# Loads of x traced inside another block, and one down group of layer 0 with two instead of three pairs in seven products

## The chip, the core and the metric

One core of a Trainium2 chip runs the whole program in one launch. The metric is the device time of one execution in microseconds (us). Most executions of a kernel lie close together; the three runs of the kernel before lie between 2137.33 and 2138.62 us, with a median of 2138.08 us.

The core has five engines with a queue of instructions each: TensorE (PE, matrix products), VectorE (DVE), ScalarE (ACT), GpSimd (POOL) and SyncE (SP, which here issues the loads of the weights). Each queue is worked off in its order, and an instruction at the head that waits holds everything behind it.

## The reference, cut to what matters

Two layers on 256 tokens of width 2048, in float32. Each layer is RMSNorm, a mixer and a residual add, then RMSNorm, a SwiGLU feed-forward and a residual add. Layer 0 mixes by sliding-window attention and an mLSTM, layer 1 by forgetting attention.

```python
for layer in range(DEPTH):
    xn = rms_norm(h, norm_mix[layer])
    mix = swa_mlstm_mixer(xn, ...) if layer % 2 == 0 else forgetting_attention_mixer(xn, ...)
    h = h + mix
    h = h + swiglu(rms_norm(h, norm_ffn[layer]), w_gate[layer], w_up[layer], w_down[layer])
return rms_norm(h, norm_final)

def swiglu(xn, w_gate, w_up, w_down):
    return (jax.nn.silu(xn @ w_gate) * (xn @ w_up)) @ w_down
```

The hidden width of the feed-forward is 5632. All weights are read from memory once, mostly 512 KB at a time.

## The kernel before, in words

**Three matmuls per product.** A float32 operand is split into a rounded part `hi` and a rest `lo`, and each product becomes three matmuls (L356 to L358, or L177 to L179 in the plain loop `gemm`): hi by xh, lo by xh, hi by xl. A weight chunk of 256 rows by 512 columns (two blocks of 128 rows, here two k's) is loaded by SP into a tile `raw` (L104), cast on ACT to `hi` (L149), and DVE forms `lo = raw - hi` (L150). `raw` tiles come from two pools of four buffers: `wr` for chunks that are only cast, and the pool `fp` of the layer for chunks of the pairs described next. `hi` and `lo` have six buffers each.

**Seven products for eight.** In the feed-forward, `pair_group` (from L373) works on two column blocks of weights at once, over a list of pairs of k's. The list (`ORDER` or `DOWN`) says for every pair whether it is plain (kind 0) or not (kind 1). A plain pair has two k's, two column blocks and two halves of 128 tokens: eight products, 24 matmuls. A pair of kind 1 forms seven products from sums of the operands: 21 matmuls, but DVE also makes `t4` (L394, L395), two blocks of `raw` (L399, L400) and splits of these (`ht`, `lt`, L251 and L252) with ACT. Four of the seven products collect in four accumulators of their own, `prods`. Behind the last pair of kind 1 these are folded once for the group: ACT copies one (L420), DVE makes `u2` and three rows of `c` (L421 to L424). What is plain collects in four other accumulators, `plain`.

**The down projection** of a part is two calls of `pair_group`, n0 = 0 and n0 = 2, for output columns 0 to 1023 and 1024 to 2047. The last part of a layer has sixteen k's, so `DOWN[8]`: eight pairs, those with numbers 2, 4 and 6 of kind 1. After each call DVE adds `c` to the residual `h` (L538, four adds of 128x512), and `close` adds the `plain` accumulators (`add_out`, L257, four adds), TensorE transposes the new `h` (`split_scaled`, L229, eight per column block of 512), ACT and DVE scale and split the transposes into `xh` and `xl` (L234, L235), and ACT forms the sums of squares (`square_sum`, L200). The next layer's first projection reads these `xh` and `xl`: its k's 0 to 7 come from the call n0 = 0, its k's 8 to 15 from the call n0 = 2. This first projection has 272 columns, the ones behind it 512.

**Order.** Python only traces the instructions. A list scheduler then orders every engine's queue by its own estimate of when operands are ready, so matmuls of the next layer's first projection stand among and behind the last of a down group. `tc.issue_after(ins)` puts each instruction of its block that runs on the same engine as `ins` behind it in that engine's queue. It sets an order and no wait. `latest[0]` is the last cast of a weight chunk, on ACT (L149).

**The start.** SP loads the transposed input in four pieces (L114) with the first four weight chunks between them, then the input itself into `h` in four pieces (L564), then weights. The squares of `h` (L200) follow on ACT. The projections `acc0` (k and v) and `acc1` (the first of q, L563 to L566) run on PE.

Of the kernel before, what the change touches and what calls it, by code (L numbers as in the profile page):

```python
# [23 lines left out]
NB = 512  # L24
# [13 lines left out]
    6: ((0, 0), (0, 1), (1, 2), (0, 3), (1, 4), (0, 5)),  # L38
    8: ((0, 0), (0, 1), (1, 2), (0, 3), (1, 4), (0, 5), (1, 6), (0, 7)),
}  # L40
MID = 6
MID_DOWN = 5
RAWS = 4
# [10 lines left out]
def trunk(  # L54
# [20 lines left out]
    nc = tc.nc  # L75
# [34 lines left out]
    h = cp.tile([P, NT, D], F32, name="h")  # L110
    xv = x[0].rearrange("(t p) d -> p t d", p=P)
# [28 lines left out]
    latest = [None]  # L140

    def load_chunk(w, k0, c0, n):
        raw = ahead.pop(0) if ahead else load_raw(w, k0, c0, n)
        return split_chunk(raw, n)
# [10 lines left out]
    def new_acc():  # L155
        return [pa.tile([P, NB], F32, tag="acc", name="acc") for _ in range(NT)]
# [6 lines left out]
    def gemm(acc, lhs, w, c0, n, k_from, k_to, k_all, skew=1):  # L163
        k0 = k_from
        while k0 < k_to:
            last = k_to == k_all and k0 + skew * CK >= k_all
            chunks = [load_chunk(w, kc, c0, n) for kc in range(k0, k_all if last else k0 + CK, CK)]
            order = [(i, t) for i in range(len(chunks) * CK) for t in range(NT)]
            if last:
                order.sort(key=lambda it: it[1])  # L170
            for i, t in order:
                k = k0 + i
                hi, lo = (c[:, i % CK, 0:n] for c in chunks[i // CK])
                ah, al = lhs(k)
                ts = slice(t * P, (t + 1) * P)
                o = acc[t][:, 0:n]
                nc.tensor.matmul(o, ah[:, ts], hi, start=(k == 0), stop=False)  # L177
                nc.tensor.matmul(o, ah[:, ts], lo, start=False, stop=False)  # L178
                nc.tensor.matmul(o, al[:, ts], hi, start=False, stop=(k == k_all - 1))  # L179
            k0 += len(chunks) * CK  # L180
# [14 lines left out]
    def square_sum(key, n):  # L195
        if n == 0:
            sums[key] = sm.tile([P, NT, 4], F32, tag="ss", name="ss")
        for t in range(NT):
            junk = sm.tile([P, NB], BF16, tag="junk", name="junk", bufs=1)
            nc.scalar.activation(  # L200
                junk, h[:, t, n * NB : (n + 1) * NB], AF.Square, accum_out=sums[key][:, t, n : n + 1]
            )

    def rstd(key):
        tot = sm.tile([P, NT], F32, tag="tot", name="tot")
        nc.vector.reduce_sum(tot, sums[key], axis=AX)
        nc.vector.tensor_scalar(tot, tot, 1.0 / D, EPS, op0=ALU.mult, op1=ALU.add)
        r = sm.tile([P, NT], F32, tag="r", name="r")
        nc.gpsimd.tensor_tensor(out=r, in0=tot, in1=mhalf[:, 0:NT], op=ALU.pow)
        return r  # L210
# [216 lines left out]
    def ffn(layer, fp, sx, sd, key, idx_next=None, key_next=None, finish=None):  # L427
# [6 lines left out]
        for g0, g1 in zip(PARTS, PARTS[1:]):  # L434
            end = g1 == PARTS[-1]
            nk = 4 * (g1 - g0)
            order = DOWN[nk // 2]
            todo = []
            for g in range(g0, g1):
# [4 lines left out]
                todo = []  # L444
# [53 lines left out]

                todo = [(MID if g < g1 - 1 else MID_DOWN, join)]

# [4 lines left out]
            def close(acc, n):  # L505
                if not end:
                    add_out(acc, n)
                elif idx_next is None:
                    finish(acc, n, gf)
                else:  # L510
                    add_out(acc, n)
                    split_scaled(idx_next, n)
                    square_sum(key_next, n)

            gf = None
            wd = w_down[layer][4 * g0 * P : 4 * g1 * P, :]
            for n0 in (0, 2):
                if end and idx_next is None and n0 == 2:
                    for n in (2, 3):
                        acc = new_acc()  # L520
                        gemm(acc, m_of, wd, n * NB, NB, 0, nk, nk, skew=3 if n == 3 else 1)
                        close(acc, n)
                    continue
                plain, c = pair_group(
                    fp, 1 - n0 // 2, m_of, sums_d, [(wd, n0 * NB), (wd, (n0 + 1) * NB)], order, todo
                )
                todo = []
                if end and idx_next is None:
                    gf = [fp.tile([P, CK, NB], F32, tag="raw", name="gf", bufs=RAWS) for _ in range(2)]
                    for i in range(2):  # L530
                        nc.gpsimd.dma_start(
                            gf[i].rearrange("p a n -> p (a n)"),
                            norm_final[i * CK * NB : (i + 1) * CK * NB].partition_broadcast(P),
                        )
                for m in range(2):
                    for t in range(NT):
                        o = h[:, t, (n0 + m) * NB : (n0 + m + 1) * NB]
                        nc.vector.tensor_tensor(out=o, in0=c[:, 2 * m + t, :], in1=o, op=ALU.add)  # L538
                for m in range(2):
                    close(plain[m], n0 + m)  # L540

    def close_layer(layer, w_out, idx, key, **rest):
        with tc.tile_pool(name=f"fp{layer}", bufs=2) as fp:
            nx = len(mixed_of(ORDER))
            nd = max(len(mixed_of(o)) for o in DOWN.values())
            sx = [fp.tile([P, nx, 4, P], F32R, name=f"sx{i}", bufs=1) for i in range(2)]
            sd = [fp.tile([P, nd, 4, P], F32R, name=f"sd{i}", bufs=1) for i in range(2)]
            out_proj(w_out, idx, key, (*sx, fp))
            ffn(layer, fp, sx, sd, key, **rest)
# [11 lines left out]
    early.close()  # L561
    acc1 = new_acc()
    for n in range(4):  # L563
        nc.sync.dma_start(h[:, :, n * NB : (n + 1) * NB], xv[:, :, n * NB : (n + 1) * NB])  # L564
        gemm(acc1, x_of, wi, OFF_QS, NB, 4 * n, 4 * n + 4, KT)
        square_sum("m0", n)  # L566
    r = rstd("m0")
    with tc.tile_pool(name="ev", bufs=1) as ev:
# [413 lines left out]
```

## Time and profile before

| | us |
|---|---|
| median of three runs | 2138.08 |
| lowest and highest | 2137.33, 2138.62 |
| the profiled execution, its own time | 2137.85 |
| its span, first to last instruction | 2136.1 |
| ACT busy in it | 1253.7 |
| DVE busy in it | 1713.8 |

The profile is of one execution. "Busy" for PE counts a matmul until its modelled end, and matmuls overlap, so what matters is the distance between their starts. In a row of a timeline the columns are start, duration, engine, line, operation, out<-in with shapes, a count, and in brackets the idle time before it and what ended that. A row with a count above one stands for several instructions in a row. In the view of waits the columns are who waited, for whom, total us, times and the longest. The granted clock is the share of its full clock that TensorE was given.

### The profile page before, as it was taken

To read this page: it belongs to the slowest core of one execution; us is meant where nothing else is said; L and a number is where in the kernel's file an instruction comes from. 1 tells how busy PE (TensorE), PEld (TensorE's weight loads), DVE (VectorE), ACT (ScalarE), POOL (GpSimd) and SP (SyncE) were. 2 spreads that over 40 slices of the span, in tenths; PEclk is the share of its full clock that TensorE was granted. 3 is DMA by queue.
4 is the path that set the end of the run, shared out by engine and by line. 5 is a ranking of instruction groups with operands and counts; after the bars stand their busy time and mean duration, and the time that the engine had idled before them with its cause. 6 is when DMAs were issued, how large, how long until landed. Compare 5 with 4: busy or idle time off the path is not lost.

```text
span 2136.1 us, 26792 instructions
## 1 busy us (share of the span) xinstructions
PE 2109.5 (99%) x9705; PEld 1752.1 (82%) x9705; DVE 1713.8 (80%) x2210; ACT 1253.7 (59%) x1594; POOL 36.7 (2%) x61
## 2 busy tenths in 40 slices
PE   7999999999999999999999999999999999999998
PEld 6888888888888888888888888888888888888886
DVE  5666567899999999999755555768899998999995
ACT  6475455665477646766545444556655667556763
POOL 2010000000000000000010000000000000000000
PEclk9999999999999999999999999999999999999999
DMA  8455556665677666766475664756766767666764
GB/s 288 137 161 163 170 188 202 203 216 181 213 211 218 211 201 212 221 214 197 139 232 165 177 177 132 235 175 187 225 198 202 233 189 208 229 201 205 223 205 135
DMA packets 257846, 420.95 MB, mean 197 GB/s; under 512 B 56449, under 2 KB 64689, under 8 KB 257585
## 3 DMA queue, kind: packets, MB, share of 16 engines
q1 hardware_dynamic: 256832, 415.49, 62.9%
q0 software_dynamic: 736, 3.71, 0.6%
q8 instruction: 76, 1.25, 0.2%
q14 instruction: 58, 0.47, 0.1%
q10 hardware_dynamic: 144, 0.03, 0.0%
HBM read 406.57 MB, written 2.11 MB: 191 GB/s over the span
## 4 chain that ended last, share of the span: by engine, by line
PE 97%; DMA 1%; DVE 1%; ACT 1%; issue 0%; SPq 0%; POOLq 0%; POOL 0%; DVEq 0%; ACTq 0%
PE acc L356 16%; PE acc L357 16%; PE acc L358 16%; PE acc L179 11%; PE acc L178 10%; PE acc L177 10%; PE prod L358 4%; PE prod L356 4%; PE prod L357 4%; PE p L280 1%; PE ptm L263 1%; PE po L331 1%; DMA xc<-in_xt_dram 1%; PE pt L229 1%; DMA raw<-in_w_up_dram 0%
## 5 line engine op out<-in xcount | busy, mean ns | idle before, releaser
L149 ACT CAST hi<-raw 128x1024 fp32r<-128x1024 f32 (+2 forms) x681 | 694.7, 1032 | 583.2 <-PE acc L179 257.7
L150 DVE TENSOR_TENSOR lo<-raw,hi 128x1024 fp32r<-128x1024 f32 (+2 forms) x681 | 809.8, 1201 | 249.3 <-ACT hi L149 247.7
L357 PE MATMUL acc<-lo,xh 128*128 128x512 f32 x946 | 368.4, 389 | 0.0
L356 PE MATMUL acc<-hi,xh 128*128 128x512 f32 x946 | 365.3, 390 | 0.3 <-DVE u L421 0.2
L358 PE MATMUL acc<-hi,xl 128*128 128x512 f32 x946 | 363.5, 389 | 0.0
L177 PE MATMUL acc<-hi,xh 128*128 128x512 f32 (+3 forms) x736 | 277.7, 380 | 12.1 <-ACT hi L149 12.1
L178 PE MATMUL acc<-lo,xh 128*128 128x512 f32 (+3 forms) x736 | 277.8, 378 | 0.6 <-DVE lo L150 0.5
L179 PE MATMUL acc<-hi,xl 128*128 128x512 f32 (+3 forms) x736 | 278.3, 379 | 0.0
L356 PEld LDWEIGHTS acc<-hi,xh 128*128 128x128 f32 x946 | 177.6, 188 | 37.9 <-DVE u L421 1.1
L358 PEld LDWEIGHTS acc<-hi,xl 128*128 128x128 f32 x946 | 177.6, 188 | 36.9
L357 PEld LDWEIGHTS acc<-lo,xh 128*128 128x128 f32 x946 | 177.6, 188 | 36.6
L357 PE MATMUL acc<-lo,mh 128*128 128x512 f32 x437 | 170.5, 390 | 0.0
L177 PEld LDWEIGHTS acc<-hi,xh 128*128 128x128 f32 x736 | 140.5, 191 | 36.2 <-ACT hi L149 12.8
L358 PE MATMUL acc<-hi,ml 128*128 128x512 f32 x437 | 168.6, 390 | 0.0
L356 PE MATMUL acc<-hi,mh 128*128 128x512 f32 x437 | 167.4, 390 | 0.0
L178 PEld LDWEIGHTS acc<-lo,xh 128*128 128x128 f32 x736 | 140.7, 191 | 25.6 <-DVE lo L150 1.7
L179 PEld LDWEIGHTS acc<-hi,xl 128*128 128x128 f32 x736 | 140.6, 191 | 25.7 <-issue 1.7
L251 ACT CAST ht<-raw 128x1024 fp32r<-128x1024 f32 x95 | 99.8, 1051 | 52.1 <-issue 20.8
L252 DVE TENSOR_TENSOR lt<-raw,ht 128x1024 fp32r<-128x1024 f32 x95 | 115.9, 1220 | 16.2 <-ACT ht L251 15.9
L177 PE MATMUL acc<-hi,mh 128*128 128x512 f32 x320 | 125.8, 393 | 1.2 <-ACT mh L251 1.2
L178 PE MATMUL acc<-lo,mh 128*128 128x512 f32 x320 | 125.8, 394 | 0.0
L179 PE MATMUL acc<-hi,ml 128*128 128x512 f32 x320 | 124.1, 390 | 0.0
(307 smaller groups left out, 3089.6 us busy)
## 6 DMA issues: line engine op xcount, KB each, us to landing
raw<-in_w_gate_dram SPq DMA_DIRECT2D x176, 512.0 KB, 4.5
raw<-in_w_up_dram SPq DMA_DIRECT2D x176, 512.0 KB, 4.7
raw<-in_w_down_dram SPq DMA_DIRECT2D x176, 512.0 KB, 4.8
raw<-in_w_in_odd_dram SPq DMA_DIRECT2D x88, 512.0 KB, 3.8
raw<-in_w_in_even_dram SPq DMA_DIRECT2D x64, 512.0 KB, 4.4
raw<-in_w_out_even_dram SPq DMA_DIRECT2D x32, 512.0 KB, 3.8
raw<-in_w_out_odd_dram SPq DMA_DIRECT2D x32, 512.0 KB, 4.0
raw<-in_w_in_odd_dram SPq DMA_DIRECT2D x8, 272.0 KB, 3.0
```

Of the source, the lines that this page charges most:

```text
L149: latest[0] = nc.scalar.copy(hi[:, :, 0:n], raw[:, :, 0:n])
L150: nc.vector.tensor_tensor(out=lo[:, :, 0:n], in0=raw[:, :, 0:n], in1=hi[:, :, 0:n].bitcast(F32), op=ALU.subtract)
L177: nc.tensor.matmul(o, ah[:, ts], hi, start=(k == 0), stop=False)
L178: nc.tensor.matmul(o, ah[:, ts], lo, start=False, stop=False)
L179: nc.tensor.matmul(o, al[:, ts], hi, start=False, stop=(k == k_all - 1))
L229: nc.tensor.transpose(pt[:, i, t, :], h[:, t, k * P : (k + 1) * P], ident)
L251: nc.scalar.copy(dst_h, src)
L252: nc.vector.tensor_tensor(out=dst_l, in0=src, in1=dst_h.bitcast(F32), op=ALU.subtract)
L263: nc.tensor.transpose(pt[:, i, :], s_, ident)
L356: nc.tensor.matmul(o, ah, hi, start=start, stop=False)
L357: nc.tensor.matmul(o, ah, lo, start=False, stop=False)
L358: nc.tensor.matmul(o, al, hi, start=False, stop=stop)
```

## The change

Two edits. In the projection `acc1` the load of a quarter of x into `h` is traced behind the matmuls of that quarter, in a block `tc.issue_after(latest[0].ins)`, where before it was traced ahead of them. And the call n0 = 2 of the last down group of layer 0 gets a list of its own, `DOWN_END`, in which pair 6 is plain: pairs 2 and 4 stay in seven products. (Layer 1's last group does not take this path for n0 = 2.)

```diff
+DOWN_END = ((0, 0), (0, 1), (1, 2), (0, 3), (1, 4), (0, 5), (0, 6), (0, 7))
...
                 plain, c = pair_group(
-                    fp, 1 - n0 // 2, m_of, sums_d, [(wd, n0 * NB), (wd, (n0 + 1) * NB)], order, todo
+                    fp,
+                    1 - n0 // 2,
+                    m_of,
+                    sums_d,
+                    [(wd, n0 * NB), (wd, (n0 + 1) * NB)],
+                    DOWN_END if end and n0 == 2 else order,
+                    todo,
                 )
...
     for n in range(4):
-        nc.sync.dma_start(h[:, :, n * NB : (n + 1) * NB], xv[:, :, n * NB : (n + 1) * NB])
         gemm(acc1, x_of, wi, OFF_QS, NB, 4 * n, 4 * n + 4, KT)
+        with tc.issue_after(latest[0].ins):
+            nc.sync.dma_start(h[:, :, n * NB : (n + 1) * NB], xv[:, :, n * NB : (n + 1) * NB])
         square_sum("m0", n)
```

The activation sums of pair 6 are still made, since the call n0 = 0 uses them.

## The prediction

> **What bounds the kernel now.** I read the page first, then the view of PE's waits, then the timelines of PE and DVE where that view points.
>
> ```profile
> PE 2109.5 (99%) x9705; PEld 1752.1 (82%) x9705; DVE 1713.8 (80%) x2210; ACT 1253.7 (59%) x1594; POOL 36.7 (2%) x61
> PE 97%; DMA 1%; DVE 1%; ACT 1%; issue 0%; SPq 0%; POOLq 0%; POOL 0%; DVEq 0%; ACTq 0%
> ```
>
> PE is busy 99% of the span, and the chain that ended last runs 97% over PE. So time changes only where PE gets more or fewer matmuls, or where one of its few waits goes. All waits of PE:
>
> ```profile
> PE acc L177 <- ACT hi L149: 12.1, 2, 7.6
> PE pt L229 <- DVE h L257: 3.8, 1, 3.8
> PE acc L177 <- ACT mh L251: 1.2, 1, 1.2
> PE acc L178 <- DVE lo L150: 0.5, 1, 0.5
> PE acc L356 <- DVE u L421: 0.2, 1, 0.2
> ```
>
> The first row is the start. The second is one wait of 3.8 us: transposes of the new residual wait for DVE's add. It lies at the end of layer 0's last down group, where the second edit is. PE there:
>
> ```profile
> 1035.63 0.39 PE L356 MATMUL acc<-hi,mh 128*128 128x512 f32 x1
> ...
> 1036.76 0.39 PE L358 MATMUL acc<-hi,ml 128*128 128x512 f32 x1
> ...
> 1037.86 0.28 PE L177 MATMUL acc<-hi,xh 128*128 128x272 f32 x1
> ...
> 1038.48 0.29 PE L179 MATMUL acc<-hi,xl 128*128 128x272 f32 x1
> ...
> 1042.23 0.39 PE L358 MATMUL prod<-ht,sd 128*128 128x512 f32 x1
> ...
> 1044.27 0.27 PE L229 MATMUL pt<-ident,h 128*128 128x128 f32 x1
> 1048.36 1.54 PE L229 MATMUL pt<-ident,h 128*128 128x128 f32 x6 [3.82 <-DVE h L257]
> 1049.56 0.57 PE L177 MATMUL acc<-hi,xh 128*128 128x272 f32 x1
> ...
> 1053.55 0.43 PE L179 MATMUL acc<-hi,xl 128*128 128x272 f32 x1
> 1053.78 0.53 PE L229 MATMUL pt<-ident,h 128*128 128x128 f32 x2
> 1054.06 0.38 PE L177 MATMUL acc<-hi,xh 128*128 128x272 f32 x1
> ```
>
> Starts give the pitch. From 1035.63 to 1036.76 lie five steps: 0.226 us for a matmul of 512 columns. From 1037.86 to 1038.48 lie five steps: 0.124 us for 272 columns. Behind the wait the same 272-column matmuls, eighteen from 1049.56 to 1053.55, stand 0.235 us apart. TensorE runs there at about half pace, as the granted clock says:
>
> ```profile
> 1040.00:1050.00 10.00, 6.18 (x31) 5.19 (x31) 7.00 (x12) 2.07 (x5) 0.00 (x0) 0.86 0.35 98
> 1050.00:1060.00 10.00, 10.00 (x65) 9.88 (x65) 8.27 (x15) 8.96 (x17) 0.69 (x1) 0.80 0.58 168
> ```
>
> The clock is the third number from the right: 0.86, then 0.80. So the wait costs twice. From 1044.27 to 1054.06 PE does 9 transposes and 18 matmuls in 9.79 us. At full pace the transposes take 0.11 us each (row below, six in 0.66) and the matmuls 0.124 us, together 9 x 0.11 + 18 x 0.124 = 3.22 us. The loss is **6.57 us**: some 3.9 of standing still and 2.7 of half pace.
>
> ```profile
> 1054.69 0.66 PE pt L229 x6
> ```
>
> Why DVE is late:
>
> ```profile
> 1042.66 0.69 DVE L421 TENSOR_TENSOR u<-prod,c 128x512 f32<-128x512 f32 x1 [3.57 <-PE prod L358]
> ...
> 1045.19 1.28 DVE L538 TENSOR_TENSOR h<-c,h 128x512 f32<-128x512 f32 x2
> 1046.39 0.72 DVE L150 TENSOR_TENSOR lo<-raw,hi 128x544 fp32r<-128x544 f32 x1
> 1047.02 0.68 DVE L538 TENSOR_TENSOR h<-c,h 128x512 f32<-128x512 f32 x1
> 1047.62 1.88 DVE L257 TENSOR_TENSOR h<-acc,h 128x512 f32<-128x512 f32 x3
> ```
>
> DVE had idled 3.57 us for the last product of pair 6 (PE's row at 1042.23, ended 1042.62). Only then can it fold the products and add, one 0.6 us step behind the other. PE has 1.7 us of matmuls left at that point.
>
> **The second edit, part by part.** With pair 6 plain, the issue lists of the two built programs are the same on PE up to the matmul at
>
> ```profile
> 1024.98 0.39 PE L356 MATMUL prod<-hi,mh 128*128 128x512 f32 x1
> ```
>
> and part there. From there to the group's last matmul before has 71 matmuls of the group, with 24 of the next projection strewn in; after has 74 in one piece. *Added:* 3 matmuls, 3 x 0.226 = **0.68 us**. Bounds: 0.68 if PE never waits, 0 if they fill a wait; I take 0.68.
>
> *Moved:* the last matmul that goes into the four products is now the 50th of those 74, for pair 4 ends it. It starts at 1024.98 + 49 x 0.226 = 1036.05 and ends at about 1036.45, where before it was 1042.62. DVE can fold at 1036.5. In its new list, from `u` (L421) to the last add stand 13 steps: ten folds and adds and three 272-column splits among them. By the rows above the first add came 2.53 us behind `u`, and that add with the eight steps behind it, at 0.6 to 0.64 us each, ends 8.1 us behind `u`, at 1044.6. PE finishes the group at 1024.98 + 74 x 0.226 = 1041.7. Then its list has 2 transposes (their adds and product buffers are through by 1039.1), 24 matmuls of 272 columns (to 1044.9), 2 transposes, 8 matmuls (to 1046.1), then the transposes that need the add of the third step from the end (1043.4), and near 1047.4 those that need the last add (1044.6). Every wait is over some 2.7 us ahead. **What is late next:** the splits `xl` of the new k's, for the matmuls near 1049.9, which by the same walk are ready about 2 us ahead, and the later ones 1.1 us ahead. If the cast buffers come free in the least lucky order (all held to 1041.9), DVE's chain shifts by 2.3 us and PE loses about 0.5 us there.
>
> *Removed from DVE and ACT:* the weight sums of pair 6, four DVE steps of 0.6 and two splits, two ACT casts; a 512-column split and cast grow to 1024. Neither engine is on the path but for the chain above, so this is worth nothing by itself.
>
> *Loads:* pair 6's second chunk and pair 7's two move to other buffers of the pool `wr`, in the same queue order.
>
> ```profile
> 1006.83 3.31 SPq L104 DMA_DIRECT2D raw<-in_w_down_dram  x3
> ...
> 1015.58 0.37 SPq L104 DMA_DIRECT2D raw<-in_w_in_odd_dram  x1
> ...
> 1018.10 0.37 SPq L104 DMA_DIRECT2D raw<-in_w_in_odd_dram  x1
> DMA to landing us min/median/max: 2.8/3.5/5.3
> L149 ACT CAST hi<-raw 128x1024 fp32r<-128x1024 f32 x2 | 2.0, 1050 | 2.9 <-issue 2.9
> L150 DVE TENSOR_TENSOR lo<-raw,hi 128x1024 fp32r<-128x1024 f32 x6 | 7.2, 1218 | 2.6 <-ACT hi L149 2.6
> ```
>
> Before, the three issues from 1006.83 held both chunks of pair 7. After, these take the buffers that are now freed for the issues at 1015.58 and 1018.10. With the longest landing of 5.3 us they are there by 1020.9 and 1023.4, cast (1.05) and split (1.22) by 1026 at the latest. PE needs the first at 1024.98 + 26 x 0.226 = 1030.9. About 5 us are to spare, so I cost this at nothing.
>
> **The first edit.** `issue_after` sets an order on the engine of the instruction it names, which is ACT. The loads of x are issued by SP. The list of the built program shows them at rows 9 to 12 of SP's queue with the same waits, ahead of all weights of this projection, before and after. A wait on the casts could not stand there, as the casts' own weights queue behind. ACT's list is the same too: the eight squares still precede the casts.
>
> ```profile
> 5.16 7.08 SPq L564 DMA_DIRECT2D h<-in_x_dram  x4
> 19.07 0.62 ACT L200 ACTIVATE junk<-h 128x512 bf16<-128x512 f32 x1
> 24.97 1.98 ACT L149 CAST hi<-raw 128x1024 fp32r<-128x1024 f32 x2
> ```
>
> Were the squares (19.07 to 24.97) to leave the casts' way, up to 5.9 us would go; were each of four loads to stop the queue for one landing, up to 4 x 5.3 = 21 us would come. I take 0, since the order is unchanged.
>
> **Sum.** Against the profiled execution (span 2136.1, its time 2137.85): -6.57 + 0.68 = -5.9 us, a span near 2130.2. The median 2138.08 is 0.2 above the profiled one; from it I predict **2132.2 us**.
>
> **A rule weighed.** The half pace lasted from 1048.36 to 1054.06, 5.7 us, after a gap of 3.8 us. The Trainium skill, "TensorE: Matmul & The Clock Gate", section "What's actually happening", says that about 3.4 us without work halve the clock, about 3.4 us of sustained work restore it, and that the windows run freely. By its figure the half pace would cost an estimated 1.7 us, not 2.7, and the sum would be 2133.2; the trace's rows decide, and I keep 2.7.
>
> **The rivals.**
> - *Another wait takes the place.* DVE's chain holds three splits, each behind an ACT cast that waits for a buffer PE frees. If these or `xl` come later than walked, PE waits again at the transposes or at the first new k's: against it stand margins of 1.1 to 2.7 us, for it that I infer the buffers. A new wait of 1 to 4 us gives 2133.2 to 2136.2, say 2134.5.
> - *The clock was lost in the profiled run only.* If the halving depends on where a 3.8 us gap falls, the runs behind the median may not have paid the 2.7 us, and only 3.9 - 0.7 = 3.2 us go: 2134.9. By the rule of free windows of some 3.4 us (the Trainium skill, same page and section) it would be so, since a gap of 3.8 us seldom holds a whole window. Against it: the profiled run at 2137.85 lies within three runs that spread by 1.3 us, less than 2.7.
> - *Slower: pair 7's weights arrive late.* They are issued up to 8.8 us later than before (1006.83 to 1015.58). Cast and split (2.3 us) must end by 1032.3 for the second, issued at 1018.1, so from a landing time of about 12 us PE stops and each further us costs one; past 18 us the 5.9 us gained are eaten. At 20 us, with the half pace of 2.7 us behind it, 2143. Landings in this window are at most 5.3 us.
> - *The first edit acts after all*, in a way that the lists don't show: -5.9 to +21 us by the bounds above, say 2128.
>
> **Chances.** Forecast 0.73; another wait 0.12; clock 0.06; late weights 0.05; first edit 0.04. A measurement here can tell about 0.2%, 4.3 us, from no change. Faster: nearly all of the forecast (0.71), a third of another wait (0.04) and half of the first edit (0.02), 0.77. Same: 0.02 + 0.08 + 0.06 = 0.16. Slower: late weights and the other half, 0.07. The forecast's own range is 2130.9 (the three matmuls cost nothing, or a run at the low end of the scatter of 0.7) to 2133.4 (0.5 lost at `xl`, scatter). To hold 8 in 10 it reaches into the first rival: 2130.9 to 2134.6.
>
> **What would show it.** In the profile after: PE's wait of 3.8 us is gone from the view of waits; the clock is 1.00 in the stretch from 1030 to 1060; PE has three matmuls more; DVE's `u` of this group starts near 1036.5; the start to 35 us is as before. A PE wait of over 1 us near 1042 to 1052, or a clock below 1, makes the first rival; a median near 2135 with no wait left makes the second.

## The result, and the profile after

| | before | after |
|---|---|---|
| median of nine runs each, one chip, us | 2137.33 | 2132.1 |
| lowest and highest, us | 2136.32, 2138.62 | 2131.22, 2132.69 |
| span of the profiled execution, us | 2136.1 | 2130.8 |

The ratio of after to before is 0.9975, with an interval of 0.9965 to 0.9985: about 0.25% faster, 5.2 us by the medians and 5.3 us by the spans. The forecast was 2132.2 us, by a gain of 5.9.

The page's row of engines and its chain that ended last, for the kernel after:

```profile
PE 2108.0 (99%) x9708; PEld 1749.6 (82%) x9708; DVE 1709.9 (80%) x2204; ACT 1252.5 (59%) x1592; POOL 35.7 (2%) x61
PE 98%; DMA 1%; ACT 1%; DVE 0%; issue 0%; SPq 0%; DVEq 0%; POOLq 0%; POOL 0%; ACTq 0%
```

PE has 9708 matmuls where it had 9705: the three that a plain pair 6 adds. DVE has six instructions fewer (four weight sums, two splits), ACT two casts fewer. PE's busy time is nonetheless 1.5 us lower with three matmuls more, because a matmul at half pace counts as longer. The waits of PE, all of them (line numbers are one higher than before up to L525, seven or eight higher behind that):

```profile
PE acc L178 <- ACT hi L150: 12.4, 2, 7.5
PE acc L178 <- ACT mh L252: 1.2, 1, 1.2
PE acc L357 <- DVE u L422: 0.3, 1, 0.3
PE acc L179 <- DVE lo L151: 0.2, 1, 0.2
```

The row of 3.8 us (`pt` behind DVE's `h`) is gone and no row has come in its place. The stretches of the kernel after around that place; the clock is the third number from the right:

```profile
1030.00:1040.00 10.00, 10.00 (x46) 8.29 (x45) 6.04 (x9) 2.94 (x5) 0.00 (x0) 1.00 0.22 63
1040.00:1050.00 10.00, 10.00 (x75) 9.52 (x74) 8.77 (x18) 7.37 (x17) 0.69 (x1) 1.00 0.63 166
1050.00:1060.00 10.00, 10.00 (x68) 9.31 (x67) 7.86 (x10) 6.74 (x9) 0.00 (x0) 1.00 0.90 261
```

Before, PE was busy 6.18 of the ten us behind 1040 and the clock read 0.86 and then 0.80. Now PE is busy throughout and the clock is 1.00. Timelines of the kernel after, DVE first, then PE:

```profile
1037.12 0.69 DVE L422 TENSOR_TENSOR u<-prod,c 128x512 f32<-128x512 f32 x1 [3.39 <-PE prod L359]
...
1042.72 1.28 DVE L258 TENSOR_TENSOR h<-acc,h 128x512 f32<-128x512 f32 x2
...
1044.55 0.69 DVE L258 TENSOR_TENSOR h<-acc,h 128x512 f32<-128x512 f32 x1
```

```profile
1025.58 0.39 PE L357 MATMUL prod<-ht,sd 128*128 128x512 f32 x1
...
1036.69 0.39 PE L359 MATMUL prod<-ht,sd 128*128 128x512 f32 x1
...
1042.13 0.39 PE L359 MATMUL acc<-hi,ml 128*128 128x512 f32 x1
1042.36 0.38 PE L230 MATMUL pt<-ident,h 128*128 128x128 f32 x2
...
1046.81 0.82 PE L230 MATMUL pt<-ident,h 128*128 128x128 f32 x6
...
1048.10 0.82 PE L230 MATMUL pt<-ident,h 128*128 128x128 f32 x6
```

DVE still idles 3.39 us for the last of the four products, but that product now ends at 1037.08 and not at 1042.62, with 24 matmuls of 512 columns still to run. The add that the transposes at 1046.81 need ends at 1044.00, the last add at 1045.24 against transposes at 1048.10: some 2.8 us of margin at both.

To separate this place from the rest of the run I take two marks on PE that every kernel here has: the first transpose of the group before (near 1000) and the first transpose `pp` of layer 1 (near 1214). Before, then after:

```profile
999.75 0.27 PE L229 MATMUL pt<-ident,h 128*128 128x128 f32 x1
...
1219.61 0.27 PE L323 MATMUL pp<-ident,s 128*128 128x128 f32 x1
```

```profile
1000.36 0.27 PE L230 MATMUL pt<-ident,h 128*128 128x128 f32 x1
...
1214.19 0.27 PE L324 MATMUL pp<-ident,s 128*128 128x128 f32 x1
```

From mark to mark before takes 219.86 us and after 213.83: 6.03 us are gained between these marks. The spans differ by 5.3 only, since after is 0.61 us late already at the first mark. The edits did not do this: the second acts behind that mark, and the kernel with the first edit alone (e1 below, whose queues are those of before) reaches it at 1000.34. What made after late shows in stretches of one us near 195 us, first of before, then of after:

```profile
195.00:196.00 1.00, 1.00 (x8) 0.70 (x7) 1.00 (x6) 0.77 (x3) 0.00 (x0) 1.00 0.53 203
```

```profile
195.00:196.00 1.00, 1.00 (x5) 0.82 (x5) 1.00 (x3) 0.90 (x4) 0.00 (x0) 0.77 0.08 16
...
198.00:199.00 1.00, 1.00 (x6) 1.00 (x5) 0.95 (x1) 0.01 (x1) 0.00 (x0) 0.53 0.00 0
```

In after the clock is at half from 195.54 to 198.94, and by the profile PE is busy in the whole stretch and in the 3.4 us ahead of it; in before the clock stays at 1.00 there. The same matmuls start 0.81 us earlier in after than in before ahead of this stretch (191.24 against 192.05) and 0.78 us later behind it (199.50 against 198.72). So a half-clock stretch can come without a gap, and not in every execution: e1 has this one too, with the queues of before.

### The profile page after: what moved, and what is told of

Its sections match the earlier page's. It is cut to its first block, busy times and chain, and to the rows that moved or that the text cites. A ratio compares the mean times of both kernels' runs of the same rounds, so it can differ in the third digit from the quotient of the medians.

```text
span 2130.8 us, 26787 instructions
## 1 busy us (share of the span) xinstructions
PE 2108.0 (99%) x9708; PEld 1749.6 (82%) x9708; DVE 1709.9 (80%) x2204; ACT 1252.5 (59%) x1592; POOL 35.7 (2%) x61
## 4 chain that ended last, share of the span: by engine, by line
PE 98%; DMA 1%; ACT 1%; DVE 0%; issue 0%; SPq 0%; DVEq 0%; POOLq 0%; POOL 0%; ACTq 0%
PE acc L357 17%; PE acc L358 17%; PE acc L359 17%; PE acc L180 11%; PE acc L178 11%; PE acc L179 10%; PE prod L357 4%; PE prod L358 4%; PE prod L359 4%; PE ptm L264 1%; PE p L281 1%; PE po L332 1%; DMA xc<-in_xt_dram 1%; PE pt L230 0%; PE pp L324 0%; PE p L274 0%
```

## The experiments

The theory under test: the second edit gives the whole gain, because the last product of the last pair of kind 1 comes early enough for DVE's chain to end before PE needs it, and the first edit does nothing. Rivals: the first edit has a part in it; the gain is less work on DVE or other loads, not the place of the last product; the half pace is a fixed price of the wait, or it is a matter of chance.

### Each edit alone

**e1**, the first edit only:

```diff
-                    DOWN_END if end and n0 == 2 else order,
+                    order,
```

> The first edit alone, the down group as before. Theory (the order block binds only instructions of ACT, and the loads of x are SP's): every queue stands as before, so the time is that of before, near 2137.3 us, with the start to 35 us unchanged. Rival (the loads of x move after all): a time at least 1 us away from before, with another start.

Measured: 2137.36 us, ratio to before 1.0001 [0.9992, 1.001]. The order of every engine's queue is that of the kernel before. The first edit is inert.

**e2**, the second edit only (the loads of x traced ahead of the matmuls as before):

> The second edit alone, the loads of x traced where they were. Theory (all of the gain comes from the end of layer 0): the time of the changed kernel, 2132.1 us, 5.2 below before. Rival (the two edits share it): a time between 2133 and 2137.

Measured: 2132.25 us, ratio 0.9978 [0.9969, 0.9987]; after was 2132.1. The second edit is the whole change. From mark to mark e2 takes 213.84 us:

```profile
1000.13 0.27 PE L230 MATMUL pt<-ident,h 128*128 128x128 f32 x1
...
1213.97 0.27 PE L324 MATMUL pp<-ident,s 128*128 128x128 f32 x1
```

The profile of e1 shows one thing more. It does the same work as the kernel before and waits as long at the same place, yet it lost less there:

```profile
PE pt L230 <- DVE h L258: 3.8, 1, 3.8
```

```profile
1000.34 0.27 PE L230 MATMUL pt<-ident,h 128*128 128x128 f32 x1
...
1044.87 0.27 PE L230 MATMUL pt<-ident,h 128*128 128x128 f32 x1
1048.96 1.54 PE L230 MATMUL pt<-ident,h 128*128 128x128 f32 x6 [3.82 <-DVE h L258]
...
1053.23 0.38 PE L230 MATMUL pt<-ident,h 128*128 128x128 f32 x2
1053.37 0.37 PE L178 MATMUL acc<-hi,xh 128*128 128x272 f32 x1
...
1218.92 0.27 PE L324 MATMUL pp<-ident,s 128*128 128x128 f32 x1
```

From 1044.87 to 1053.37 are 8.50 us for the same nine transposes and 18 matmuls that took 9.79 us in the profile before, and mark to mark are 218.58 us, not 219.86. The wait is 3.82 us in both; what differs is how long the clock stayed at half. One-us stretches show its edges, first of before, then of e1:

```profile
1047.00:1048.00 1.00, 0.00 (x0) 0.00 (x0) 1.00 (x3) 0.00 (x0) 0.00 (x0) 0.63 0.00 0
...
1054.00:1055.00 1.00, 1.00 (x10) 1.00 (x10) 0.06 (x1) 0.98 (x1) 0.00 (x0) 0.96 0.79 117
```

```profile
1048.00:1049.00 1.00, 0.04 (x1) 0.05 (x1) 1.00 (x3) 0.01 (x1) 0.00 (x0) 0.69 0.30 23
...
1051.00:1052.00 1.00, 1.00 (x7) 1.00 (x7) 0.50 (x2) 1.00 (x4) 0.00 (x0) 0.61 0.01 4
```

All stretches between read 0.50. A mean of 0.63 over one us is 0.26 us at full clock and 0.74 at half, so before was halved from 1047.26 to 1054.08 (0.96 leaves 0.08 at half), 6.82 us; e1, in the same way, from 1048.38 to 1051.78, 3.40 us. One is twice the other.

### How early the last product has to be

**e3**, pair 2 alone of kind 1 (three more matmuls than after, and the last product earlier still):

```diff
-DOWN_END = ((0, 0), (0, 1), (1, 2), (0, 3), (1, 4), (0, 5), (0, 6), (0, 7))
+DOWN_END = ((0, 0), (0, 1), (1, 2), (0, 3), (0, 4), (0, 5), (0, 6), (0, 7))
```

> The list of the last down group of layer 0 with pair 2 alone in seven products, pairs 4 and 6 plain. Theory (the gain is the wait, which is gone already; each plain pair costs three matmuls of 0.226 us): 0.7 us above the changed kernel, about 2132.8. Rival (the gain comes from less work on DVE, of which more now goes): below the changed kernel, about 2130.

Measured: 2132.56 us, ratio 0.9979 [0.997, 0.9988], 0.3 us above e2 and 0.5 above after. From mark to mark (999.75 to 1214.37) it takes 214.62 us, 0.79 above after: the three matmuls cost what 3 x 0.226 = 0.68 says, near enough, and nothing is gained by being earlier than after already is. Nor does still less work on DVE gain anything, as the rival had it.

**e4**, three pairs of kind 1, placed earlier in the list:

```diff
+DOWN_END = ((0, 0), (1, 2), (0, 1), (1, 4), (0, 3), (1, 6), (0, 5), (0, 7))
```

> All three pairs in seven products, but at places 1, 3 and 5 of eight, with two plain pairs behind the last. Theory (what matters is how many matmuls stand behind the last product that goes into the sums, not how many pairs are in seven): no PE wait at the transposes, three matmuls less than the changed kernel, 0.7 us below it, about 2131.4. Rival (three pairs of kind 1 make DVE late wherever they stand): a wait of 2 to 4 us is back and the time is 2134 to 2138.

Measured: 2133.26 us, ratio 0.9981 [0.9972, 0.999], where 2131.4 was expected. The scheduler still puts the products of pair 6 late, with 14 matmuls of 512 columns of the group behind the last of them (8 before, 24 after), and PE waits. The waits of e4, and its clock in the ten us in which it does:

```profile
PE pt L230 <- DVE h L258: 1.1, 1, 1.1
```

```profile
1040.00:1050.00 10.00, 8.95 (x59) 8.02 (x57) 9.03 (x16) 4.73 (x12) 0.00 (x0) 1.00 0.45 123
```

No half clock came with a wait of 1.1 us: the clock stays 1.00.

**e5**, pair 6 of kind 1 at the place of pair 5:

```diff
+DOWN_END = ((0, 0), (0, 1), (1, 2), (0, 3), (1, 4), (1, 6), (0, 5), (0, 7))
```

> Three pairs in seven products at places 2, 4 and 5, two plain pairs behind them. Theory (matmuls behind the last product decide): between before and the changed kernel; pair 4 and pair 6 follow each other, so DVE makes the sums of pair 6 under pressure; if the last product ends 2 us earlier than in before, the wait shrinks from 3.8 to about 1.8 us and the half pace goes, about 2133.5 us. Rival (the scheduler puts the same matmuls last whatever the list says): 2137, as before.

Measured: 2136.1 us, ratio 0.9993 [0.9984, 1.0002], where about 2133.5 was expected. About three quarters of the gain is gone. PE waits 2.5 us, in its timeline here, and the clock is halved from 1049.24 to 1052.64, 3.40 us, by the one-us stretches behind it:

```profile
1047.82 0.87 PE L230 MATMUL pt<-ident,h 128*128 128x128 f32 x6 [2.46 <-DVE h L258]
```

```profile
1049.00:1050.00 1.00, 1.00 (x8) 1.00 (x7) 1.00 (x4) 1.00 (x4) 0.00 (x0) 0.62 0.88 270
...
1052.00:1053.00 1.00, 1.00 (x8) 1.00 (x7) 0.99 (x2) 1.00 (x2) 0.26 (x1) 0.68 0.81 98
```

The transposes at 1047.82 still ran at full pace (0.87 us for six, in e1 1.54), so here the halving came while PE was working again.

The number of matmuls alone does not decide, as the theory had it: e4 and e5 both have 14 of 512 columns behind the last product, and wait 1.05 and 2.46 us. What differs is the time that PE can fill. From the start of the last product to the first transpose it is 2.04 us in before, 3.40 in e5 and 4.58 in e4, where nine matmuls of the next projection stand there as well. With the waits (3.82, 2.46 and 1.05) the sums are 5.86, 5.86 and 5.63 us. In after PE has 5.67 us there and does not wait.

### A later DVE with the new list

If the margin at the adds is what matters, the new list with more work on DVE must wait again. **e6** and **e7** add 8 and 12 steps ahead of the adds; each takes the maximum of a row of `c` with itself, which leaves it as it is:

```diff
+                if end and n0 == 2:
+                    for _ in range(8):
+                        nc.vector.tensor_tensor(out=c[:, 1, :], in0=c[:, 1, :], in1=c[:, 1, :], op=ALU.max)
                 for m in range(2):
```

> The changed kernel with eight steps of 0.6 us (a maximum of one row of c with itself) put on DVE ahead of the residual adds of the last down group of layer 0. DVE's adds come 4.8 us later, against some 2.7 us of cover: a PE wait of about 2 us at the transposes. Theory (half pace comes only behind a wait of over some 3 us): the wait alone is lost, about 2134.1 us, granted clock 1.00 behind it. Rival (every wait is followed by half pace in proportion, 0.7 us for each us): about 2135.5, clock below 1.

> The same with twelve such steps: adds 7.2 us later, a PE wait of about 4.4 us. Theory: the wait and a half pace of about 2.7 us behind it, about 2139.2 us, clock near 0.8 in the 10 us behind the wait. Rival (no half pace, the 2.7 us of before had another cause): about 2136.5, clock 1.00.

Measured: e6 2138.64 us, ratio 1.0007 [0.9997, 1.0016], where 2134.1 was expected; e7 2142.51 us, ratio 1.0023 [1.0014, 1.0033], where 2139.2 was expected. The scheduler spread the steps among DVE's other work, so the wait came later than meant and others of 0.8 to 1.0 us came with it. What gates PE is the same pair of lines. PE's transposes at the wait in e6, then in e7:

```profile
1056.82 1.50 PE L230 MATMUL pt<-ident,h 128*128 128x128 f32 x6 [2.02 <-DVE h L258]
```

```profile
1059.27 1.54 PE L230 MATMUL pt<-ident,h 128*128 128x128 f32 x6 [4.92 <-DVE h L258]
```

The edges of the half clock in e6:

```profile
1056.00:1057.00 1.00, 0.18 (x1) 0.18 (x2) 0.73 (x2) 0.20 (x1) 0.00 (x0) 0.95 0.50 188
...
1060.00:1061.00 1.00, 1.00 (x6) 0.77 (x5) 1.00 (x3) 0.78 (x3) 0.69 (x1) 0.84 0.00 0
```

It lasts from 1056.90 to 1060.32, 3.42 us, behind a wait of only 2.0 us. My expectation that half pace follows only waits of more than about 3 us is refuted. In e7 the same reading gives 1056.60 to 1063.44, 6.84 us. So the new list is fast because DVE's chain is through in time; late DVE steps alone bring the wait and the half clock back, and take the whole gain (e6, whose interval holds 1) or more (e7).

### The loads of x where they do act

The first edit names a cast on ACT, so it cannot move a load on SP. **e8** names the last weight load instead:

```diff
+    loaded = [None]
...
-        nc.sync.dma_start(
+        loaded[0] = nc.sync.dma_start(
...
-        with tc.issue_after(latest[0].ins):
+        with tc.issue_after(loaded[0].ins):
```

> The changed kernel with the four loads of x really moved: each is put behind the last weight load of its quarter in SP's queue (the block names the load, not the cast). The squares on ACT then follow the casts. Theory (the PE wait of 4.9 us near 21 us is there because the casts stand behind the eight squares and their weights behind the loads of x): that wait and the half pace behind it shrink, 3 to 8 us below the changed kernel, 2124 to 2129. Rival (the start is bound by what must be loaded, whatever its order, or the later scale factors make the heads wait): within 1 us of the changed kernel, or above it.

Measured: **2125.2 us**, ratio to before 0.994 [0.9928, 0.9953], 6.9 us below after. This is the fastest version by its median; its five executions lie between 2122.92 and 2126.21 us. SP's queue in the kernel after, then in e8:

```profile
5.12 7.13 SPq L573 DMA_DIRECT2D h<-in_x_dram  x4
13.30 0.61 SPq L105 DMA_DIRECT2D raw<-in_w_in_even_dram  x1
```

```profile
8.91 14.34 SPq L107 DMA_DIRECT2D raw<-in_w_in_even_dram  x6
23.30 0.46 SPq L575 DMA_DIRECT2D h<-in_x_dram  x1
```

In after, four loads of x stand ahead of the weights that `acc1` needs; in e8, six weight loads go first. The first 35 us of after and of e8:

```profile
0.00:35.00 35.00, 22.27 (x75) 16.47 (x76) 18.83 (x30) 23.93 (x44) 12.38 (x31) 0.90 0.92 307
```

```profile
0.00:35.00 35.00, 27.28 (x109) 21.86 (x110) 20.46 (x28) 21.72 (x34) 14.53 (x30) 1.00 0.91 311
```

PE runs 109 matmuls there, not 75. After waits 4.93 us for a cast up to 26.07, and its mean clock of 0.90 stands for 7 of the 35 us at half; e8 has neither. The DMA engines are as busy in both (0.92 and 0.91): the same bytes, in an order that PE can use.

**e9** moves the squares of `h` on ACT behind the casts instead, and leaves the loads in front:

```diff
+        nc.sync.dma_start(h[:, :, n * NB : (n + 1) * NB], xv[:, :, n * NB : (n + 1) * NB])
         gemm(acc1, x_of, wi, OFF_QS, NB, 4 * n, 4 * n + 4, KT)
         with tc.issue_after(latest[0].ins):
-            nc.sync.dma_start(h[:, :, n * NB : (n + 1) * NB], xv[:, :, n * NB : (n + 1) * NB])
-        square_sum("m0", n)
+            square_sum("m0", n)
```

> The changed kernel with the loads of x back ahead, and the squares on ACT, instead of the loads, traced in the block that names the cast (the same engine, so the order holds). ACT then casts the weights of the first projection of q before it squares x. Theory (both orders matter at the start: 5.9 us of squares, and weights that land late behind four loads of x): part of the gain of the kernel with the loads moved, about 2128 to 2131 us. Rival (the loads' order alone makes the start): within 0.5 us of 2132.1.

Measured: 2131.0 us, ratio 0.9972 [0.9961, 0.9984], 1.1 us below after. The executions of the two overlap (2130.03 to 2132.06 here, 2131.22 to 2132.69 for after), so this is a small gain at most. The cast no longer stands behind squares, but then it waits for its weights; ACT in e9:

```profile
23.75 1.04 ACT L150 CAST hi<-raw 128x1024 fp32r<-128x1024 f32 x1 [4.75 <-DMA raw<-in_w_in_even_dram]
```

It starts at 23.75, where before it started at 24.97, and PE waits 3.45 us for it and 0.53 for a split, where after waited 4.93. So the loads of x hold the weights, and that is most of what e8 removes.

**e10** is e8 with the old list, and **e11** is e8 with three pairs of kind 1 placed earlier still:

```diff
-DOWN_END = ((0, 0), (0, 1), (1, 2), (0, 3), (1, 4), (0, 5), (0, 6), (0, 7))
+DOWN_END = ((0, 0), (1, 2), (1, 4), (0, 1), (1, 6), (0, 3), (0, 5), (0, 7))
```

> The loads of x really moved, with the old list (three pairs, at places 2, 4 and 6). Theory (start and end of layer 0 are independent): the gain of the move, 6.9 us, off the time of before, about 2130.4 us, with the wait of 3.8 us at the transposes back. Rival (the gain of the move is in part the end's): about 2132 or more, or a wait of another size.

> The loads of x really moved, and three pairs in seven products at places 1, 2 and 4 of eight. In the order of the built program 20 matmuls of 512 columns stand behind the last product (24 in the changed kernel, 14 where three pairs left a wait of 1.1 or 2.5 us, 8 in before). Theory (that number decides): no wait at the transposes, three matmuls less, 0.7 us below the kernel with the loads moved, about 2124.5 us. Rival (three pairs always bring a wait): 2126 to 2129, wait of over 1 us.

e10: 2130.82 us, ratio 0.9971 [0.996, 0.9983]. The wait is back, and the list is worth 2130.82 - 2125.2 = 5.6 us here, against 5.2 between before and after. The two places are 1000 us apart, and their gains add within the scatter of e8. PE's wait in e10:

```profile
PE pt L232 <- DVE h L260: 3.8, 1, 3.8
```

e11: 2127.64 us, ratio 0.9954 [0.994, 0.9967], where 2124.5 was expected; it is 2.4 us above e8, with executions (2125.11 to 2128.37) that overlap those of e8. Of its waits, the one that e8 has not:

```profile
PE acc L360 <- DVE lo L153: 1.1, 2, 0.7
```

The wait at the transposes is gone here too (20 matmuls of the group stand behind the last product), but PE waits 1.1 us for two of DVE's splits of weights, near 1004 and 1010, more than the 0.68 that three matmuls fewer save. DVE is busy there for 19.43 of the 20 us from 1000 to 1020, in e8 for 17.98; that the sums of three pairs, now early in the group, fill it is argued and not shown. Of the span's 2.1 us over e8, 1.05 were there ahead of the first mark (993.75 against 992.70), and 1.2 came between the marks; about 0.8 of these I have not traced, and the same 0.7 or so is unexplained in e4.

## Why the prediction was right

**The place and the mechanism.** The wait of 3.8 us is gone, the clock is 1.00, PE has three matmuls more, and the start is unchanged: 22.30 us of PE in the first 35 before, 22.27 after, all as predicted. The walk of the changed order held. Measured from its own start, which came 0.60 us later than in the profile before (1025.58 against 1024.98), `u` started at 1036.52 (forecast 1036.5), the group ended at 1041.76 (1041.7), the last add at 1044.64 (1044.6), and the two runs of transposes began at 1046.21 and 1047.50 (1046.1 and 1047.4).

**The cost.** Three matmuls were put at 0.68 us; e3, with three more, took 0.79 more from mark to mark.

**The first edit at nothing.** e1 shows it: 1.0001 [0.9992, 1.001]. The bounds for moving the squares and the loads were up to 5.9 us gained and up to 21 us lost. Moved for certain, the squares alone gave about 1 at most (e9) and loads and squares together 6.9 (e8): the feared stop for landings did not come, since in e8 a load of x is issued right behind the weight loads ahead of it (at 23.30, as 8.91 + 14.34 ends).

**The size of the half pace, the term that was mis-sized.** The forecast took 2.7 us of half pace as the price of the wait, from one profile. That price is not fixed: with the same wait, e1 paid 8.50 - 3.22 - 3.9 = 1.4 us. Its loss is 5.28 us, before's 6.57, so the second edit is worth 4.6 or 5.9 us, by the run. The marks say the same: before to after is 6.03 us, e1 to e2 is 218.58 - 213.84 = 4.74 us. The measured 5.2 lies between. The forecast time still came out within 0.1 us, since the median of three runs that it started from (2138.08) was 0.75 above the median of nine (2137.33): two small errors of opposite sign. That it came so close is luck.

**The rule that was weighed.** The lengths of the half clock come in two sizes: 3.40 (e1, e5), 3.42 (e6), and 6.82 (before, e10), 6.84 (e7). This agrees with the free-running windows of about 3.4 us that the Trainium skill, "TensorE: Matmul & The Clock Gate", section "What's actually happening", describes; the forecast had read it as one window only. Its other clause, that about 3.4 us without work halve the clock, is not what these runs show as a condition on the gap: the clock was halved behind gaps of 2.0 (e6) and 2.5 us (e5), and not behind 1.1 us (e4), and near 195 us in after it was halved behind no gap at all. The sum by the rule that was weighed, 2133.2 or a gain of 4.9 us, lies nearer to the measured 5.2 than the forecast's 5.9; by e1 and before, neither size is paid in every execution.

**The rivals.** No other wait took the place (after's list of waits). Pair 7's weights were in time (no wait of PE on them). The rival that the clock was lost in the profiled run alone was half true: half clock was paid at this place in every profile with the old list (before, e1, e10), at one of two sizes. Its 2134.9 would have needed none.

## What to carry to other kernels

When PE is 99% busy, look for its one wait and for what the awaited chain starts with: three matmuls at 0.23 us each were a good price for ending the last folded product 24 matmuls ahead of the group's end instead of 8. The margin to leave is more than the wait that one sees, since at this place the clock was halved as well with gaps of 2.0 to 4.9 us, for 3.4 or 6.8 us, and which of the two differs from run to run; so price a gap from several profiles. And an ordering block acts only on the queue of the engine that it names: look at the built order before giving such an edit a gain or a cost.

## What the runs showed of the hardware that was not expected

- The half clock came in two lengths, one twice the other. Every half-clock stretch read here lasted 3.40 to 3.42 or 6.82 to 6.84 us, whatever the gap before it: 3.82 us of waiting gave 6.82 in before and 3.40 in e1.
- The start of a half-clock stretch need not fall in the gap. In e5 PE had been running again for 1.4 us (from 1047.82) when the clock was halved at 1049.24.
- A gap of 2.0 us went with it in e6, and near 195 us no gap was needed: in after the clock was at half from 195.54 to 198.94 with PE busy, in before it was not. Just ahead, from 192.55 to 194.52, PE runs eight matmuls on four rows each (`pb` from `mt` and `sel`); that they bring it is not shown.
